# Hybrid attention and retention layer on one core: merged probabilities in dilation 1, and two reordered seams

## The chip, the core and the metric

The kernel runs on one core of a Trainium2 chip. Its engines work side by side, each through a queue of its own in order: TensorE (PE, matrix products and transposes; PEld is its weight load), VectorE (DVE), ScalarE (ACT), GpSimd (POOL) and SyncE (SP, which here only issues DMA transfers). The metric is the device time of one execution in microseconds (us).

## The reference

One decoder layer over 4096 positions of width 1024: RMSNorm, one input projection, two groups of heads, SiLU gates, one output projection, a residual add and a final RMSNorm. The part that the change touches is the dilated attention:

```python
ATTN_HEADS = 8; ATTN_HEAD_DIM = 64
DILATED_BRANCHES = ((128, 1), (512, 4), (2048, 16))

def dilated_branch(q, k, v, window, dilation):
    # query t attends t, t-d, t-2d, ..., t-window
    steps = window // dilation                      # 128 in each branch
    ...
    s = jnp.einsum('bhrnqd,bhrnkd->bhrnqk', qb, kb) * (Dh ** -0.5)
    dist = steps + qi - kj
    band = (dist >= 0) & (dist <= steps)            # 129 keys, over this block and the one before
    ...
    m = jnp.max(s, axis=-1, keepdims=True)
    p = jnp.exp(s - m)
    den = jnp.sum(p, axis=-1, keepdims=True)
    o = jnp.einsum('bhrnqk,bhrnkd->bhrnqd', p, vb) / den
    lse = (m + jnp.log(den))[..., 0]

def dilated_attention(q, k, v):
    ...
    w = jax.nn.softmax(jnp.stack(lses, axis=0), axis=0)
    o = jnp.sum(w[..., None] * jnp.stack(outs, axis=0), axis=0)
```

A key at distance 128 is in the band of dilation 1 (its 129th key) and in that of dilation 4 as well, and counts once in each.

Beside it stand four retention heads (chunks of 128, a running state), their GroupNorm, and `mixed = concat(silu(ga) * attn, silu(gr) * ret); mixed @ w_out`. All of it is float32; the large products are done as three products of split numbers (a high part and a rest), `mm3`.

## The kernel before

There are three phases. Phase 1 (to about 753 us) computes the projections, rotates q and k, and stores q, k, v to DRAM. Phase 2 (to about 1668 us) computes the attention and the retention. Phase 3 computes the gates, mixes the branches by their weights, projects and normalises. In phases 1 and 2 each engine's order is the order in which the code is written; in phase 3 a scheduler sets it.

**Phase 2.** A head is worked off in 24 items: four of dilation 1, eight of dilation 4, eight of dilation 16, four of dilation 1. An item is four blocks of 128 queries in two banks (halves) of two blocks. `attention()` runs over half-slots t, and `yield`s the modelled PE cost of each; the loop around it puts pieces of `filler()` (the retention and its value projection, 32 chunks) between them until the modelled time of a slot is full. Half-slot t issues, for one half of an item:

- PE: `qk_bank`, the scores S of half t (L667; two buffers in PSUM), then `t_bank`, transposes of the probabilities P of half t-2 (L704), then every second half-slot `pv_group` of the item from four half-slots before (L737);
- ACT: `o_copy` (L752), `exp_row` twice for half t-1 (L695), and for the second half of an item `t_copy`, the transposed tile T into half of `pt` (L714);
- DVE: `row_max` twice for half t (L688: adds the mask, finds the row's extreme, writes it to nm), and for the first half of an item `t_copy` (L716).

A block's P is 128 queries by 256 keys: the block before and its own. So an item has eight 128x128 transposes, less one for a block without a predecessor. `pt` has eight slots of 128x128, and there are two such tiles.

**Seam 1**, between phases 1 and 2. `store_values` multiplies v by the row scale on ACT (vo, L274) and issues its stores to DRAM from ACT's own queue (L276 to L283). The filler's first products V (L49 to L51) need a split chunk of the input: hi on ACT (L433), the rest on POOL (L434). A finished V is copied out by ACT (vch, L1036).

**Seam 2**, between phases 2 and 3. The statistics of all heads are in `raw`, and `branch_weights` turns them into weights for the three branches; heads 0 to 5 in phase 2 on DVE, heads 6 and 7 at the start of phase 3 on POOL (L516 to L528), with M and the reciprocal on DVE (L512, L513, L525) and the exponential on ACT (L518). There the weights of the output projection are split as well: hi by ACT, the rest by POOL and DVE in turn (wo, L89). The gates' first values are e (ACT, then DVE L1191), m is their split (ACT L41, DVE L42), and po the output projection.

## Time and profile before

| | us |
|---|---|
| median of 3 runs (lowest, highest) | 2422.44 (2421.32, 2423.11) |
| the profiled execution, its own time | 2423.84 |
| its span, first instruction to last | 2422.0 |
| busy in it: PE, DVE, ACT, POOL | 2340.4, 1468.1, 994.5, 732.9 |

The profile shows one execution. Busy times are sums over the span; the times from start to end are the first two rows. A group of instructions has its line, engine, operation, output and inputs by their names in the program, count, busy time and mean length in ns, then the idle time ahead of it and what ended that.

### The profile page before, as it was taken

How to read it: one execution, taken by the hardware profiler on the slowest of the kernel's cores; microseconds unless marked ns; L12 is line 12 of the kernel's file. 1: busy time of each engine (PE TensorE's matmuls, PEld its weight loads, DVE VectorE, ACT ScalarE, POOL GpSimd, SP SyncE). 2: the span in 40 equal slices, each digit the busy share in tenths (PEclk: the TensorE clock that was granted, in tenths of full speed). 3: DMA queues.
4: the chain of work that ended last, by engine and by line, in shares of the span. 5: the costliest groups of instructions: out<-in, count | busy, mean ns of one | idle time of the engine just before them, and what ended most of it. 6: DMA issues, size and time to landing. Idle time of an engine off the chain costs nothing. (4 is left out here: it accounts for less than half of the span.)

```text
span 2422.0 us, 41800 instructions
## 1 busy us (share of the span) xinstructions
PE 2340.4 (97%) x14568; PEld 1983.6 (82%) x14568; DVE 1468.1 (61%) x3908; ACT 994.5 (41%) x2870; POOL 732.9 (30%) x774
## 2 busy tenths in 40 slices
PE   7999999999997999999999999997899999999998
PEld 5778888888885888888888888876788999989997
DVE  5643443443433878787887879774665565565554
ACT  4322212212202666667666666666222222222221
POOL 5312112112112545344543535447221121121110
PEclk9999999999998999999999999999899999999999
DMA  6343343343356665758575665754676666666563
GB/s 191 129 146 125 116 142 126 118 142 124 119 170 190 162 156 138 186 128 195 136 175 149 151 168 123 184 144 157 152 167 161 144 164 159 140 159 162 144 156 92
DMA packets 404259, 362.59 MB, mean 150 GB/s; under 512 B 191848, under 2 KB 334824, under 8 KB 398928
## 3 DMA queue, kind: packets, MB, share of 16 engines
q1 hardware_dynamic: 389408, 332.91, 51.9%
q10 hardware_dynamic: 14112, 25.43, 3.4%
q8 instruction: 115, 1.88, 0.3%
q0 software_dynamic: 528, 1.58, 0.2%
q14 instruction: 96, 0.79, 0.1%
HBM read 241.18 MB, written 118.64 MB: 149 GB/s over the span
## 5 line engine op out<-in xcount | busy, mean ns | idle before, releaser
L688 DVE CUSTOM_DVE_ANT_0 S<-S,mask 128x256 f32<-128x256 f32 (+1 forms) x768 | 308.6, 402 | 159.8 <-PE S L667 124.8
L695 ACT ACTIVATE P<-S,nm 128x256 f32<-128x256 f32 (+1 forms) x768 | 337.8, 449 | 41.1 <-DVE nm L688 37.6
L51 PE MATMUL g<-h,wg 128*128 128x256 f32 x1024 | 289.9, 283 | 0.0
L704 PE MATMUL T<-ident,P 128*128 128x128 f32 x1368 | 213.7, 274 | 0.0
L50 PE MATMUL po<-wo,m 128*128 128x512 f32 x512 | 202.1, 395 | 3.0 <-POOL wo L89 2.0
L51 PEld LDWEIGHTS g<-h,wg 128*128 128x128 f32 x1024 | 196.8, 192 | 0.1
L737 PE MATMUL O<-pt,v 128*64 128x128 f32 (+1 forms) x1968 | 196.5, 326 | 0.0
L667 PE MATMUL S<-kk,qc 128*128 128x256 f32 x1024 | 187.1, 306 | 5.8 <-issue 2.6
L49 PE MATMUL po<-wohi,m 128*128 128x512 f32 x448 | 176.2, 393 | 13.3 <-ACT m L41 10.9
L1245 POOL TENSOR_TENSOR rs<-v,mhalf 128x1 f32<-128x1 f32 x32 | 17.4, 543 | 534.0 <-DVE v L1243 392.2
L667 PEld LDWEIGHTS S<-kk,qc 128*128 128x128 f32 x1024 | 149.8, 190 | 33.5 <-issue 16.9
L51 PE MATMUL po<-wohi,m 128*128 128x512 f32 x448 | 176.5, 394 | 0.0
L173 POOL TENSOR_TENSOR sq<-sq,sq 128x512 f32<-128x512 f32 x56 | 76.1, 1360 | 326.9 <-ACT sq L169 326.9
L737 PEld LDWEIGHTS O<-pt,v 128*64 128x64 f32 x1968 | 121.4, 137 | 60.8 <-issue 31.9
L41 ACT ACTIVATE m<-e 128x256 fp32r<-128x256 f32 x128 | 53.1, 417 | 285.5 <-DVE e L1191 156.4
L704 PEld LDWEIGHTS T<-ident,P 128*128 128x128 f32 x1368 | 164.4, 142 | 0.2 <-ACT wg0hi L88 0.2
L434 POOL TENSOR_TENSOR hc<-hr,hc 128x512 fp32r<-128x512 f32 x64 | 85.3, 1334 | 243.6 <-ACT hc L433 160.7
L695 ACT ACTIVATION_READ_ACCUMULATOR P<-S,nm 128x1 f32 x768 | 157.2, 205 | 0.0
L49 PE MATMUL g<-h,wg0hi 128*128 128x256 f32 x512 | 145.4, 284 | 3.3 <-ACT e L1184 3.3
L49 PE MATMUL g<-h,wg1hi 128*128 128x256 f32 x512 | 145.4, 284 | 2.8 <-ACT e L1184 2.8
L50 PE MATMUL g<-h,wg1hi 128*128 128x256 f32 x512 | 146.1, 286 | 1.7 <-DVE h L482 1.5
L50 PE MATMUL g<-h,wg0hi 128*128 128x256 f32 x512 | 145.4, 284 | 0.0
(213 smaller groups left out, 6107.0 us busy)
## 6 DMA issues: line engine op xcount, KB each, us to landing
q<-dr_q SPq DMA_DIRECT2D x128, 256.0 KB
hr<-in_xT_dram SPq DMA_DIRECT2D x64, 512.0 KB
wb<-dr_w SPq DMA_DIRECT2D x128, 192.0 KB
o<-dr_o SPq DMA_DIRECT2D x192, 128.0 KB
v<-dr_v SPq DMA_DIRECT2D x94, 256.0 KB
xt<-in_xT_dram SPq DMA_DIRECT2D x64, 256.0 KB
dr_q<-hl SPq DMA_DIRECT2D x32, 512.0 KB
dr_k<-hl SPq DMA_DIRECT2D x32, 512.0 KB
```

What stands on the lines that cost most here:

```text
L41: nc.scalar.activation(dst[:, 0], src, AF.Copy)
L49: nc.tensor.matmul(out, wh, xh, start=first and i == 0, stop=False)
L50: nc.tensor.matmul(out, wh, xl, start=False, stop=False)
L51: nc.tensor.matmul(out, wl, xh, start=False, stop=last and i == n - 1)
L173: nc.gpsimd.tensor_tensor(sums[b], sums[b], sq, ALU.add)
L434: nc.gpsimd.tensor_tensor(hc[:, :, 1, :], src, hc[:, :, 0, :].bitcast(F32), ALU.subtract)
L667: nc.tensor.matmul(s[:, j * 256 : (j + 1) * 256], qq[h, t, half][:, off : off + 128] if br == 0 else it["q"][:, t, i, :], rhs, start=(j == ...
L688: nc.vector.tensor_tensor_reduce(sv, sv, mask[:, it["br"], c0:256], 1.0, BIG, ALU.add, ALU.min, accum_out=nm[:, col : col + 1])
L695: nc.scalar.activation(it["P", i // 2][:, i % 2, c0:256], sv, AF.Exp, bias=nm[:, col : col + 1], scale=-1.0, accum_out=den[:, col : col + 1])
L704: nc.tensor.transpose(t[:, j * 128 : (j + 1) * 128], it["P", bank][:, j // 2, j % 2 * 128 : j % 2 * 128 + 128], ident)
L737: nc.tensor.matmul(o[64 * bank : 64 * bank + 64, c0 : c0 + 128 * m], vt[h, br, idx // 8][:, idx % 8, :], it["pt"][:, a : a + m, :].rearran ...
L1245: nc.gpsimd.tensor_tensor(rs, v, mhalf, ALU.pow)
```

## The change

Four things are changed.

1. In dilation 1 (all items but the last two of the last head; 62 of 64, marked `one`), the key at distance 128 is left out of the mask, and counts twice in dilation 4 instead (its mask there is -log 2, as scores are negated). A query then has 128 keys, and at each position within a block only one of the two, the key in the block before or in its own, is allowed: so `merge` adds the two 128x128 parts of P into one, on DVE for the first bank and on POOL for the second. `t_merged` transposes the four merged parts into one tile T. `t_apart` takes them apart: ACT copies T to the even slots of `pt` (L755 in the changed kernel), DVE multiplies T by a triangle into the odd slots (L757), and POOL multiplies the even slots in place by the other triangle (L758). pv of a merged item stands two half-slots later, that of the item behind it one. P has five buffers instead of three.
2. The triangles are made at the start of phase 2 out of the mask, with one transpose.
3. Seam 1: two of the last vo tiles come from another pool, the hi parts of chunks 0 and 1 are made on DVE, chunk 0's earlier, and vch of chunks 0 and 1 is copied by DVE.
4. Seam 2: the branch weights of heads 6 and 7 are computed on DVE and spread over the first three steps of the split of wo; an unused Silu at the end of phase 2 has ACT's table loaded earlier.

```diff
@@ store_values (seam 1)
             if b + 1 == NBLK and i >= 2:
-                vf = op.tile([128, 2, BLK], F32, tag="hl", name="vo1")[:, 0, :]
+                vf = xp.tile([128, BLK], F32, tag="x", name="vo1")
@@ the last block of phase 1 (seam 1): moved from behind store_values(b, 0, p) to ahead of the splits of w2
+                ahead["hch"] = {0: [split_h_chunk(nc, hcp, raw, 0, j, nc.vector) for j in range(2)]}
+                ahead["hr"] = load_x_chunk(nc, hcp, io, 1)
...
-                    if i == 0:
-                        ahead["hch"] = {0: [split_h_chunk(nc, hcp, raw, 0, j) for j in range(2)]}
-                        ahead["hr"] = load_x_chunk(nc, hcp, io, 1)
@@ split_h_chunk
-def split_h_chunk(nc, pool, t, c, i):
+def split_h_chunk(nc, pool, t, c, i, hi=None):
 
     hc = pool.tile([128, KT // 2, 2, 128], F32R, tag=f"hc{(2 * c + i) % 3}", name="hc2")
     src = t[:, KT // 2 * i : KT // 2 * (i + 1), :]
-    nc.scalar.activation(hc[:, :, 0, :], src, AF.Copy)
+    if hi:
+        hi.tensor_copy(hc[:, :, 0, :], src)
+    else:
+        nc.scalar.activation(hc[:, :, 0, :], src, AF.Copy)
     nc.gpsimd.tensor_tensor(hc[:, :, 1, :], src, hc[:, :, 0, :].bitcast(F32), ALU.subtract)
     return hc
@@ branch_weights (seam 2): every engine.tensor_tensor becomes nc.vector.tensor_tensor
-def branch_weights(nc, dr, raw, M, h0, h1, engine=None):
+def branch_weights(nc, dr, raw, M, h0, h1):
...
-    engine.tensor_tensor(den, nm, den, ALU.mult)
+    nc.vector.tensor_tensor(den, nm, den, ALU.mult)
@@ phase2, setup
-        pp = pool("p2p", 3)
+        pp = pool("p2p", 5)
...
+        nc.vector.tensor_scalar(mask[:, 0, :128], mask[:, 0, 128:], -1.0, BIG, ALU.mult, ALU.add)
+        for half, far in ((0, 128), (1, 0)):
+            mv = mask[:, 1, half * 128 : half * 128 + 128]
+            nc.gpsimd.affine_select(
+                out=mv,
+                in_=mv,
+                compare_op=ALU.not_equal,
+                fill=-float(np.log(2.0)),
+                base=32 - far,
+                pattern=[[32, 4], [1, 4], [4, 8]],
+                channel_multiplier=-1,
+            )
+
+        tri = cp.tile([128, 2, 128], F32, name="tri2")
+        nc.vector.tensor_scalar(tri[:, 1, :], mask[:, 0, 128:], 0.0, None, ALU.is_equal)
+        trit = psT.tile([128, 512], F32, tag="T", name="tri2")
+        nc.tensor.transpose(trit[:, :128], tri[:, 1, :], ident)
+        nc.vector.tensor_copy(tri[:, 0, :], trit[:, :128])
+        nc.vector.tensor_scalar(tri[:, 1, :], trit[:, :128], -1.0, 1.0, ALU.mult, ALU.add)
@@ phase2, new helpers
+        def merge(it, bank):
+
+
+            a = 1 if it["blocks"][2 * bank][1] == 0 else 0
+            P = it["P", bank]
+            (nc.gpsimd if bank else nc.vector).tensor_tensor(P[:, a:, 128:], P[:, a:, 128:], P[:, a:, :128], ALU.add)
+
+        def t_merged(it):
+
+            t = psT.tile([128, 512], F32, tag="T", name="T2")
+            for i in range(4):
+                nc.tensor.transpose(t[:, i * 128 : (i + 1) * 128], it["P", i // 2][:, i % 2, 128:], ident)
+            it["T"] = t
+
+        def t_apart(it):
+            t = it["T"].rearrange("p (b q) -> p b q", b=4)
+            pt = it["pt"].rearrange("p (b t) q -> p b t q", t=2)
+            nc.scalar.activation(pt[:, :, 0, :], t, AF.Copy)
+            low, up = (tri[:, i].unsqueeze(1).broadcast_to([128, 4, 128]) for i in range(2))
+            nc.vector.tensor_tensor(pt[:, :, 1, :], t, low, ALU.mult)
+            nc.gpsimd.tensor_tensor(pt[:, :, 0, :], pt[:, :, 0, :], up, ALU.mult)
+
@@ phase2, items and attention()
+                it["one"] = br == 0 and not (h == H - 1 and gi >= len(groups) - 2)
+
+                it["slot"] = 2 * len(items) + (6 if it["one"] else 5 if items and items[-1]["one"] else 4)
...
+                im = im if im and im["one"] and not bm else None
+                i2 = i2 if i2 and not i2["one"] else None
+                if im:
+                    t_merged(im)
+                    cost += 4 * TRN
                 if i2:
                     cost += t_bank(i2, b2) * TRN
-                if 0 <= g < len(items):
-                    pv_group(items[g])
-                    cost += pv_cost(items[g])
-                if 0 <= gp < len(items):
-                    o_copy(items[gp])
+                for itp in by_slot.get(t - 1, ()):
+                    o_copy(itp)
+                for itp in by_slot.get(t, ()):
+                    pv_group(itp)
+                    cost += pv_cost(itp)
                 if i1:
                     exp_row(i1, 2 * b1)
                     exp_row(i1, 2 * b1 + 1)
+                    if i1["one"]:
+                        merge(i1, b1)
+                if im:
+                    t_apart(im)
@@ filler(), retention's value projection
-                        nc.scalar.activation(res[c]["vch"], pv, AF.Copy, scale=ahead["rs"][:, c : c + 1])
+                        if c < 2:
+                            nc.vector.tensor_scalar(res[c]["vch"], pv, ahead["rs"][:, c : c + 1], None, ALU.mult)
+                        else:
+                            nc.scalar.activation(res[c]["vch"], pv, AF.Copy, scale=ahead["rs"][:, c : c + 1])
@@ pacing
-            872 + TRN * (8 - sum(it["blocks"][2 * i][1] == 0 for i in range(2))) + pv_cost(it) for it in items[: len(groups)]
+            872 + TRN * (4 if it["one"] else 8 - sum(it["blocks"][2 * i][1] == 0 for i in range(2))) + pv_cost(it)
+            for it in items[: len(groups)]
@@ end of phase 2
+            if t == n + 1:
+
+                nc.scalar.activation(ahead["junk"], ahead["mhalf"], AF.Silu)
@@ start of phase 3 (seam 2)
-            for _ in branch_weights(nc, dr, raw, M, 6, 8, nc.gpsimd):
-                pass
...
+            weights = branch_weights(nc, dr, raw, M, 6, 8)
             for j in range(7):
+                for _ in range((5, 3, 4, 0, 0, 0, 0)[j]):
+                    next(weights, None)
                 wo7.split(j, None if j % 2 else nc.gpsimd)
```

Lines of the changed kernel differ: scores L687, row maxima L708, exponentials L715, transposes L724 (L749 for merged items), vch on DVE L1093, weight splits L88, mm3 L48 to L50.

**DVE in a stretch with dilation 1** (near the boundary of heads 2 and 3; S are the scores, nm the row's extremes, the rows with nm alone read out an accumulator). Before:

```order
L688 ISA S2_6912,nm2_5477<-S2_6912,mask2_5378 128x256 [waits PE_49,Activation_49]
L688 ISA nm2_5477 128x1
L688 ISA S2_6912,nm2_5477<-S2_6912,mask2_5378 128x256 [waits DVE_49]
L688 ISA nm2_5477 128x1
L716 COPY pt0_5390<-T2_6917 128x512 [waits PE_49]
L688 ISA S2_6937,nm2_5477<-S2_6937,mask2_5378 128x256 [waits PE_49,Activation_49]
L688 ISA nm2_5477 128x1
L688 ISA S2_6937,nm2_5477<-S2_6937,mask2_5378 128x256 [waits DVE_49]
```

After (stm, mv, rs and qc belong to the filler or to the next item's queries):

```order
L743 TENSOR_TENSOR P2_7039<-P2_7039 128x2x128 [waits Activation_49,Pool_49]
L708 ISA S2_7073,nm2_6965<-S2_7073,mask2_5379 128x256 [waits PE_49]
L708 ISA nm2_6965 128x1
L708 ISA S2_7073,nm2_6965<-S2_7073,mask2_5379 128x256 [waits DVE_49]
L708 ISA nm2_6965 128x1
L1052 BN_AGGR mv2_7025<-bs2_7024 128x2 x4
L1053 TENSOR_SCALAR rs2_7026<-mv2_7025 128x4 [waits DVE_49]
L988 TENSOR_TENSOR stm2_7103<-Rs2_7096,decay2_5381 128x512 [waits PE_49]
L663 COPY qc2_7109<-q2_10_6715 128x512 [waits DMAHW3_49,DMAHW7_49,DMAHW2_49,DMAHW0_49]
L757 TENSOR_TENSOR pt0_5404<-T2_7118,tri2_5398 128x4x128 [waits Activation_49]
L708 ISA S2_7113,nm2_6965<-S2_7113,mask2_5379 128x256
L708 ISA nm2_6965 128x1
```

The copy of a T tile, which waits for PE, is gone; ahead of the row maxima stands a merge or a multiplication, and each waits for ACT.

**ACT at the same place** (P are the probabilities, os the copy of a finished output, hc a chunk of the filler). Before:

```order
L695 ACTIVATE P2_6878,den2_5478<-S2_6879,nm2_5477 128x256 [waits DVE_49,Activation_49]
L695 ACTIVATE P2_6878,den2_5478<-S2_6879,nm2_5477 128x256
L752 ACTIVATE os2_6947<-O2_6922 128x256 [waits DMAHW5_49,DMAHW4_49,PE_49]
L695 ACTIVATE P2_6911,den2_5478<-S2_6912,nm2_5477 128x256 [waits DVE_49,Activation_49]
L695 ACTIVATE P2_6911,den2_5478<-S2_6912,nm2_5477 128x256
L714 ACTIVATE pt0_5390<-T2_6942 128x512 [waits PE_49]
L1016 ACTIVATE on2_6721<-Rt2_6959 128x512 [waits DMAHW2_49,PE_49]
L695 ACTIVATE P2_6936,den2_5478<-S2_6937,nm2_5477 128x256 [waits DVE_49,Activation_49]
```

After:

```order
L715 ACTIVATE P2_7039,den2_6966<-S2_7040,nm2_6965 128x256 [waits DVE_49,Activation_49]
L715 ACTIVATE P2_7039,den2_6966<-S2_7040,nm2_6965 128x256
L434 ACTIVATE hc2_7085<-hr2_6832 128x4x128
L715 ACTIVATE P2_7072,den2_6966<-S2_7073,nm2_6965 128x256 [waits DVE_49,Activation_49]
L715 ACTIVATE P2_7072,den2_6966<-S2_7073,nm2_6965 128x256
L755 ACTIVATE pt0_5404<-T2_7118 128x4x128 [waits PE_49,Pool_49]
L794 ACTIVATE os2_7146<-O2_7123 128x256 [waits DMAHW2_49,DMAHW1_49,PE_49]
L715 ACTIVATE P2_7112,den2_6966<-S2_7113,nm2_6965 128x256 [waits DVE_49,Activation_49]
```

The copy into pt stands behind the second pair of exponentials, as before, but it now takes a merged T, DVE's multiplication waits for it, and it waits for POOL.

**PE at the start of phase 2** (mm1 is phase 1's last product, V the filler's first). Before:

```order
L50 MATMUL mm1_5273<-w1v7_634,h1_4621 128x512
L51 MATMUL mm1_5273<-w1vhi_128,h1_4621 128x512
L49 MATMUL V2_5418<-w2hi_4948,hc2_5199 128x512 [waits Activation_49]
L50 MATMUL V2_5418<-w20_5142,hc2_5199 128x512 [waits DVE_49]
L51 MATMUL V2_5418<-w2hi_4948,hc2_5199 128x512 [waits Pool_49]
```

After:

```order
L49 MATMUL mm1_5273<-w1v7_634,h1_4621 128x512
L50 MATMUL mm1_5273<-w1vhi_128,h1_4621 128x512
L600 MATMUL tri2_5400<-ident2_5374,tri2_5398 128x128 [waits DVE_49,Pool_49]
L48 MATMUL V2_5432<-w2hi_4948,hc2_5138 128x512 [waits Activation_49]
L49 MATMUL V2_5432<-w20_5150,hc2_5138 128x512
```

A transpose of the triangle, which waits for DVE and POOL, stands first.

**DVE at the start of phase 3.** Before:

```order
L512 TENSOR_TENSOR M3_5322<-raw3_5321 32x256 [waits DMAHW5_49,DMAHW4_49]
L513 TENSOR_TENSOR M3_5322<-M3_5322,raw3_5321 32x256 [waits DMAHW6_49,DVE_49]
L525 RECIPROCAL M3_5322<-M3_5322 32x256 [waits Pool_49]
L89 TENSOR_TENSOR wo1_17884<-wo2_17752,wohi_17734 128x1024 [waits DMAHW2_49,DMAHW1_49,DMAHW3_49,PE_49,Activation_49]
L89 TENSOR_TENSOR wo3_17982<-wo4_17756,wohi_17734 128x1024 [waits DMAHW3_49,DMASW0_49,DMAHW4_49,Activation_49,Pool_49]
L89 TENSOR_TENSOR wo5_18109<-wo6_17760,wohi_17735 128x1024 [waits DMAHW5_49,DMAHW6_49,Activation_49,Pool_49]
```

After:

```order
L512 TENSOR_TENSOR M3_5322<-raw3_5321 32x256 [waits DMAHW5_49,DMAHW4_49]
L513 TENSOR_TENSOR M3_5322<-M3_5322,raw3_5321 32x256 [waits DMAHW6_49,DVE_49]
L516 TENSOR_TENSOR raw3_5321<-M3_5322,raw3_5321 32x256 [waits DVE_49]
L516 TENSOR_TENSOR raw3_5321<-M3_5322,raw3_5321 32x64x4
L516 TENSOR_TENSOR raw3_5321<-M3_5322,raw3_5321 32x16x16
L520 TENSOR_TENSOR raw3_5321<-raw3_5321 32x768 [waits DMAHW7_49,DMAHW0_49,Activation_49]
L522 TENSOR_TENSOR M3_5322<-raw3_5321 32x256 [waits DVE_49]
L523 TENSOR_TENSOR M3_5322<-M3_5322,raw3_5321 32x256 [waits DVE_49]
L525 RECIPROCAL M3_5322<-M3_5322 32x256 [waits DVE_49]
L88 TENSOR_TENSOR wo1_17778<-wo2_17651,wohi_17633 128x1024 [waits DMAHW1_49,DMASW7_49,DMAHW2_49,Activation_49,Pool_49]
L528 TENSOR_TENSOR raw3_5321<-raw3_5321,M3_5322 32x256 [waits DVE_49]
L528 TENSOR_TENSOR raw3_5321<-raw3_5321,M3_5322 32x256 x2
```

The operations between M and the reciprocal, which POOL had, stand in DVE's queue; the first of wo stands behind the reciprocal as before, and three of the weights' operations behind that.

More of the change, by code (lines that the diff above doesn't have):

```diff
@@ L21 @@
 HS = 5
-WAITG = 3
 REST = 6500.0
@@ L494, in gate_products @@
     )
-def branch_weights(nc, dr, raw, M, h0, h1, engine=None):
-    engine = engine or nc.vector
+def branch_weights(nc, dr, raw, M, h0, h1):
     ps = slice(16 * h0, 16 * h1)
@@ L515, in branch_weights @@
     for br in range(3):
-        engine.tensor_tensor(nat(nm, br), shp(M, br), nat(nm, br), ALU.subtract)
+        nc.vector.tensor_tensor(nat(nm, br), shp(M, br), nat(nm, br), ALU.subtract)
         yield
@@ L527, in branch_weights @@
     for br in range(3):
-        engine.tensor_tensor(shp(den[:, br, :], br), nat(nm, br), shp(M, br), ALU.mult)
+        nc.vector.tensor_tensor(shp(den[:, br, :], br), nat(nm, br), shp(M, br), ALU.mult)
         yield
@@ L821, in attention @@
             nh = 2 * len(items)
+            by_slot = {}
+            for it in items:
+                by_slot.setdefault(it["slot"], []).append(it)
             def half(t):
@@ L832, in attention @@
                 i2, b2 = half(t - 2)
-                g = (t - 4) // 2 if t % 2 == 0 else -1
-                gp = (t - 5) // 2 if t % 2 else -1
+                im, bm = half(t - 4)
                 if it and b == 0:
@@ L1049, in filler @@
                     if k == 0 and 1 <= c < NCH:
-                        hch[c].append(split_h_chunk(nc, hcp, hraw.pop(c), c, 1))
+                        hch[c].append(split_h_chunk(nc, hcp, hraw.pop(c), c, 1, nc.vector if c < 2 else None))
                     if k == HL and 1 <= c < NCH - 1:
@@ L1355, in body @@
             tc.nc.sync.dma_start(ahead["rgain"], io["ret_gain"])
+            ahead["junk"] = rawp.tile([128, 1], F32, name="junk3")
             ahead["mhalf"] = rawp.tile([128, 1], F32, name="mhalf3")
```

8 lines of the change are left out of this document (4 added, 4 removed).

## The prediction

> **What bounds the kernel now.** I read the page first, for the shares of the engines.
>
> ```profile
> span 2422.0 us, 41800 instructions
> PE 2340.4 (97%) x14568; PEld 1983.6 (82%) x14568; DVE 1468.1 (61%) x3908; ACT 994.5 (41%) x2870; POOL 732.9 (30%) x774
> ```
>
> TensorE is busy nearly all the time, so anything taken off it should count. But the share is a mean over three phases, so I next read the table of stretches over the places that the change touches: seven stretches of eight items each (an item is two half-slots, four query blocks) with dilation 1, the last four of one head and the first four of the next. The first row and the sum (busy time of each engine, then PE's clock):
>
> ```profile
> 873.90:909.90 36.00, 36.00 (x289) 30.24 (x288) 27.62 (x102) 24.30 (x82) 12.37 (x14) 1.00 0.75 181
> ...
> sum 251.50, PE 251.31 PEld 211.71 DVE 188.64 ACT 178.37 POOL 82.90; mean PE 35.90 PEld 30.24 DVE 26.95 ACT 25.48 POOL 11.84
> ```
>
> PE is busy for 251.31 of 251.50 us at full clock (the 1.00), so it is the bound there; 251.5 / 56 = 4.49 us per item. DVE has 75%, ACT 71%: neither is full, but both are full enough that the order in which they wait for one another matters. So I read the groups of instructions by line and shape (busy time, mean ns of one), and then the timeline inside one such stretch.
>
> ```profile
> L714 ACT ACTIVATE pt<-T 128x512 f32<-128x512 f32 x128 | 76.9, 601 | 10.6 <-PE T L704 10.3
> L932 DVE TENSOR_TENSOR stm<-Rs,decay 128x512 f32<-128x512 f32 x32 | 22.0, 688 | 17.3 <-PE Rs L923 17.1
> L1202 DVE TENSOR_TENSOR a<-a,u 128x256 f32<-128x256 f32 x64 | 27.0, 421 | 0.6
> L434 POOL TENSOR_TENSOR hc<-hr,hc 128x512 fp32r<-128x512 f32 x64 | 85.3, 1334 | 243.6 <-ACT hc L433 160.7 <-DVE on L1002 20.5 <-DMA q<-dr_q 20.4
> L1191 DVE SCALAR_TENSOR_TENSOR e<-rt,rgain,e 128x256 f32<-128x256 f32 x64 | 45.1, 707 | 21.6 <-ACT e L1184 16.7 <-DMA rt<-dr_ret 4.8
> ```
>
> ```profile
> 1102.59 0.47 ACT L695 ACTIVATE P<-S,nm 128x256 f32<-128x256 f32 x1
> 1102.77 0.60 PE L704 MATMUL T<-ident,P 128*128 128x128 f32 x4
> 1103.08 0.43 DVE L688 CUSTOM_DVE_ANT_0 S<-S,mask 128x256 f32<-128x256 f32 x1 [0.57 <-PE S L667]
> 1103.20 0.38 PE L942 MATMUL Rk<-ident,rk 128*128 128x128 f32 x2
> ...
> 1103.48 0.61 ACT L714 ACTIVATE pt<-T 128x512 f32<-128x512 f32 x1
> 1103.60 0.43 DVE L688 CUSTOM_DVE_ANT_0 S<-S,mask 128x256 f32<-128x256 f32 x1
> ...
> 1103.95 0.14 DVE L688 DVE_READ_ACCUMULATOR2_ANT nm<- 128x1 f32 x1
> ...
> 1104.19 0.48 ACT L695 ACTIVATE P<-S,nm 128x256 f32<-128x256 f32 x1
> ...
> 1105.01 0.20 ACT L695 ACTIVATION_READ_ACCUMULATOR P<-S,nm 128x1 f32 x1
> ```
>
> What to see: DVE starts the row maxima of one half (1103.08) while ACT is still at the exponentials of the half before (from 1102.59). They overlap: DVE waits only for PE's scores, and every copy out of T waits only for PE's transposes.
>
> **The change part by part.**
>
> *Fewer transposes.* A merged item has 4 transposes instead of 8 (7 in a head's first group). By the order of both, 240 fewer. Four in the timeline run from 1102.77 to the next PE operation at 1103.20, 0.43 us, some 0.109 each (0.43 / 4): 240 x 0.109 = 26.2 us less PE work, all of it on the path wherever PE is the bound. The filler (retention) is paced by the cost model, so this is spread over 192 items: 0.14 each. A dilation-1 item whose bound is PE would take 4.49 - 0.14 = 4.35 us.
>
> *Copies, merges and multiplications.* ACT had one copy of a T tile per item (L714, 0.60) and has one still, so nothing. POOL gets a merge of 256 columns and a multiplication in place over 512 (L434, 1.33; the merge is half as wide, so at most that): under 2.7 us per merged item. With the 33% that it has, POOL stays below a full item; its results are wanted a slot or two later, since pv moves from slot 2i+4 to 2i+6. I cost that at nothing; the cover is those two slots, and the five instead of three P buffers. DVE gets a merge of 256 columns with both inputs in SBUF (nearest L1202, 0.42) and a multiplication out of PSUM over 512 (nearest L932, 0.69) in place of a copy of the same size.
>
> *The new waits on DVE, which decide.* By the order of the changed kernel, in a merged item's odd half-slot DVE's merge (L743) stands ahead of the next row maxima, and waits for ACT's exponentials of the half before. In the even half-slot DVE's multiplication by the triangle (L757) stands ahead of the row maxima, and waits for ACT's copy (L755), which stands on ACT's queue behind the exponentials of the half before. ACT's exponentials wait for DVE's row maxima. So where DVE and ACT now overlap, they would alternate, once round per item:
> - row maxima to exponentials: 1103.08 to 1104.19, 1.11;
> - exponentials to the copy behind them: 1102.59 to 1103.48, 0.89; the copy 0.61;
> - hand-over ACT to DVE: 0.05 (ACT's vo below ends at 758.50, PE's V starts at 758.55);
> - multiplication: 0.69, the next starting 0.08 before its end (L688 at 1103.60 lasts 0.43, its successor starts 0.35 later): 0.61;
> - row maxima again 1.11; exponentials to their last result, 1104.19 to 1105.21, 1.02; hand-over 0.05; merge 0.42 - 0.08 = 0.34.
>
> Sum 5.79 us against 4.35: 1.44 more for each of the 62 merged items, 89 us. PE can run ahead by two score buffers only, so each of the 8 stretches (the first four items, seven boundaries of heads, two at the end) hides about 1 us once, 8 in all: +81. Bounds of the one unknown size, the merge: L1202's 0.42, taken as the nearest in shape and kind; above, the factor by which such an operation grew beside POOL. In the seam below, two L1191 took 2.96 us while POOL worked from 1699.34 to 1702.54, against 2 x 0.707: 2.1 times. At that, the merge costs 0.46 more, 62 x 0.46 = +28. Below, the wait is free if other work on DVE hid it: 0.
>
> The section "Who interferes with whom" of the Trainium skill's page "SBUF — State Buffer" says that a DVE instruction with two SBUF inputs and a GpSimd instruction that reads SBUF lock each other out for a whole instruction. That speaks against the merge on DVE; the 2.96 us row agrees in direction, though it shows a stretch and no full block (a full block until 1702.54 would have put the end near 1703.95, and it came at 1703.21). By that rule, with POOL's retention work (a third of the time) in the way, the merge waits up to 1.33, about 0.44 in the mean: 2488 in place of 2461.
>
> *Setup and seam 1* (start of phase 2):
>
> ```profile
> 754.10 0.78 POOL L572 DMA_DIRECT2D mask<-in_masks_dram  x1
> mask<-in_masks_dram POOLq DMA_DIRECT2D x1, 384.0 KB, 6.7
> 757.81 0.69 ACT L274 ACTIVATE vo<-mm,rs_all 128x512 f32<-128x512 f32 x1 [7.54 <-DMA dr_k<-hl]
> 758.55 0.79 PE L49 MATMUL V<-w2hi,hc 128*128 128x512 f32 x1 [4.93 <-ACT vo L274]
> 777.71 0.80 PE L49 MATMUL V<-w2hi,hc 128*128 128x512 f32 x1 [11.51 <-ACT vch L1036]
> 783.91 0.63 ACT L433 ACTIVATE hc<-hr 128x512 fp32r<-128x512 f32 x1 [5.74 <-DMA hr<-in_xT_dram]
> ```
>
> Now the triangle's transpose stands first on PE and needs the mask, which lands at 754.10 + 6.7 = 760.8; with two small DVE operations V starts near 761.7 instead of 758.55, 3.1 later. On POOL the two affine selects wait for the mask too, with the retention's first loads queued behind them: those are wanted after chunk 1, so nothing. Against it, vch of chunk 0 leaves ACT, whose queue is full of value stores, for DVE: the 11.51 us wait shrinks to about 0.8. That is 10.7 - 3.1 = 7.6, and a little more at full clock; but ACT's split of chunk 2 still waits for its load ahead of the exponentials. I take 8 us off (4 to 10).
>
> *Seam 2* (start of phase 3):
>
> ```profile
> 1669.82 1.28 ACT L1184 ACT_TABLE_LOAD   x1 [3.30 <-DMA dr_o<-os]
> 1675.22 1.04 DVE L513 TENSOR_TENSOR M<-M,raw 32x256 f32<-32x256 f32 x1
> 1679.39 0.84 ACT L518 ACTIVATE raw<-raw 32x768 f32<-32x768 f32 x1 [2.57 <-POOL raw L516]
> 1686.54 1.75 DVE L525 RECIPROCAL M<-M 32x256 f32<-32x256 f32 x1 [10.28 <-POOL M L523]
> 1688.32 1.22 DVE L89 TENSOR_TENSOR wo<-wo,wohi 128x1024 fp32r<-128x1024 f32 x1
> 1699.34 3.20 POOL L89 TENSOR_TENSOR wo<-raw,wohi 128x1024 fp32r<-128x1024 f32 x1 [1.39 <-DVE wo L89]
> 1700.25 2.96 DVE L1191 SCALAR_TENSOR_TENSOR e<-rt,rgain,e 128x256 f32<-128x256 f32 x2
> L89 POOL TENSOR_TENSOR wo<-wo,wohi 128x1024 fp32r<-128x1024 f32 x3 | 7.0, 2349 | 1.6 <-DVE wo L89 1.4
> L516 DVE TENSOR_TENSOR raw<-M,raw 96x256 f32<-96x256 f32 x3 | 2.4, 813 | 0.0
> L522 DVE TENSOR_TENSOR M<-raw 96x256 f32<-96x256 f32 x1 | 1.7, 1654 | 0.0
> ```
>
> Today the weights of heads 6 and 7 go through POOL, DVE waits 10.28 us for them, and its second e (1700.25) and PE behind it stall. All on DVE: M is ready at 1676.26, three L516 to 1678.7, ACT's exponential to 1679.5, then the product, the two sums and their like (two L522's length at most, 3.3, and half as much again for L520) to about 1683.2 to 1684.5, the reciprocal to about 1685, wo of step 1 to 1686.2 instead of 1689.54. From there POOL and DVE alternate through wo 2 to 5: 2 x 2.35 + 2 x 1.22 = 7.1, so e starts at 1693.3 instead of 1700.25, 7.0 earlier. The preloaded table saves up to 1.28 more, where PE waits for the first e. I take 8 off (5 to 11). The weights' stores go later on SP's queue than the loads of rt, but the weights themselves are ready earlier than now.
>
> *Sum.* +81 - 26 - 8 - 8 = +39. The profiled run took 2423.84, 1.84 around its span of 2422.0, and lies 1.40 above the median of the runs, 2422.44: 2463 by the profiled run, 2461 by the median, which I forecast.
>
> **The rivals.** All from the same sum; a net of zero needs 0.81 more than 4.35 per merged item ((26 + 16 + 8) / 62), a round of some 5.2 us.
>
> 1. *PE stays the bound* (the other side: faster). The waits cost nothing where DVE and ACT have slack elsewhere in the item. For it: DVE at 75% and ACT at 71%. Against: both of DVE's waits stand directly ahead of the row maxima that ACT waits for, and two score buffers don't cover 1.4 us per item again and again. It decides if the round is below 4.35. Then only the gains are left: 2422 - 26 - 16 = 2380.
> 2. *Half a chain.* If the multiplication need not wait for ACT's copy into the same pt tile, or the copy finds a gap between exponentials, 0.66 falls out: a round of 5.13, 62 x 0.78 - 8 = +40, net -2: about 2421. For it: the two write different halves of the tile. Against: the order gives the wait on ACT there.
> 3. *POOL lengthens the merge*, as bounded above: +28, 2489. For it, the L1191 row; against, that POOL's own multiplication begins together with DVE's and ends long before the merge.
> 4. *The clock falls* in stretches where PE idles. The stretch around the first seam shows it:
>
> ```profile
> 753.00:791.00 38.00, 21.56 (x95) 17.46 (x94) 6.25 (x23) 6.86 (x18) 16.59 (x21) 0.73 0.69 202
> ```
>
> There PE was busy for 57% and was granted 0.73 of its clock. In the forecast it would be busy for 4.35 / 5.79 = 75%. At half clock PE's 4.35 would be 8.7 per item; in one stretch in eight that is some 8 x 2.9 = 23 us more: about 2485 to 2510.
>
> **How the numbers follow.** Forecast (round of 5.5 to 6.0, 2443 to 2475 with the seams' bounds) 0.56; rival 1 0.12; rival 2, with rounds of 4.9 to 5.4 (2406 to 2437), 0.12; rival 3 0.14; rival 4 0.06. A difference under 0.2% (4.8 us) is about what a measurement of this kernel can't tell from none. Rival 1 and a third of rival 2 are faster, 0.16; a quarter of rival 2 and little else is no change, 0.04; slower 0.80. The range leaves out rival 1, the low end of rival 2 and the worst of rivals 3 and 4: 2412 to 2495; the forecast's own is 2443 to 2475.
>
> **What the profile after would show.** Right: in the same stretches PE's busy share falls to about 75%, an item takes 5.5 to 6 us, PE's idle time ahead of its scores (S, L687) is released by ACT's exponentials, and DVE has new idle time ahead of the merge and the multiplication released by ACT, some 62 x 2 times. L749 and L724 together have 1128 transposes. The stretches with dilation 4 and 16 get shorter by 0.14 per item. V starts near 761.7, and again for chunk 1 near 770 instead of 777.71; in phase 3 the e that starts at 1700.25 comes some 7 us earlier after M than now. Wrong would be: PE at 97% in those stretches (rival 1); idle time only ahead of the merge (rival 2); a merge above 0.6 us in the mean (rival 3); a clock below 1 there (rival 4). What would make it wrong most easily is ACT's or DVE's queue running ahead at a place where I have them wait, since the sum counts each link in full.

## The result, and the profile after

| | us |
|---|---|
| before, median of 4 runs (lowest, highest) | 2422.61 (2421.32, 2423.11) |
| after, median of 4 runs (lowest, highest) | 2487.95 (2484.29, 2489.70) |
| ratio after to before, 95% interval | 1.0268 (1.0253 to 1.0282) |
| the profiled execution after, its span | 2484.29, 2482.5 |

The change makes the kernel 65 us slower; the forecast was 2461, with 2488 inside the stated range (2412 to 2495), but above the 2443 to 2475 of the forecast's own mechanism. The profiled execution is the fastest of the four, and its span is 60.5 us longer than before's. The page's first two lines:

```profile
span 2482.5 us, 41541 instructions
PE 2341.0 (94%) x14329; PEld 1963.8 (79%) x14329; DVE 1517.2 (61%) x3989; ACT 991.5 (40%) x2865; POOL 855.5 (34%) x891
```

PE has 239 instructions fewer (240 transposes off, the triangle's one added), and yet its share of the span falls from 97 to 94%: it waits. The table of stretches over the same seven places as before, each from the first of a head's last four items to the fourth of the next head (first row, and the sum):

```profile
878.30:922.40 44.10, 35.85 (x265) 28.57 (x265) 30.46 (x110) 25.12 (x85) 29.74 (x31) 1.00 0.79 173
...
sum 310.40, PE 257.09 PEld 201.67 DVE 211.20 ACT 177.21 POOL 190.66; mean PE 36.73 PEld 28.81 DVE 30.17 ACT 25.32 POOL 27.24
```

Cut at the same scores, eight items took 35.6 us before (249.5 / 7) and take 44.3 now (310.4 / 7), with PE busy for 83%, at full clock in six of the seven, and no other engine above 68%. An engine that is full would explain the loss; none is. What PE and DVE wait for, in the views of waits (total, times, longest, us); the first row is before's, the others after's:

```profile
PE S L667 <- ACT P L695: 6.9, 8, 2.3
```

```profile
PE S L687 <- ACT P L715: 60.0, 84, 3.3
PE O L779 <- POOL pt L758: 5.2, 7, 0.9
DVE P L743 <- ACT P L715: 61.0, 54, 2.7
DVE pt L757 <- ACT pt L755: 44.4, 37, 3.7
```

PE's wait for the score buffers that ACT's exponentials free went from 6.9 to 60.0 us: 53 of the 60.5. DVE's two new waits are the merge behind the exponentials and the multiplication behind ACT's copy. One round of the loop in the timeline, with the start and length of each operation:

```profile
1140.86 0.69 DVE L757 TENSOR_TENSOR pt<-T,tri 128x512 f32<-128x512 f32 x1 [0.87 <-ACT pt L755]
1141.47 0.42 DVE L708 CUSTOM_DVE_ANT_0 S<-S,mask 128x256 f32<-128x256 f32 x1
...
1142.57 0.47 ACT L715 ACTIVATE P<-S,nm 128x256 f32<-128x256 f32 x1 [1.47 <-DVE nm L708]
...
1143.05 1.28 POOL L758 TENSOR_TENSOR pt<-pt,tri 128x512 f32<-128x512 f32 x1
...
1143.64 0.74 PE L687 MATMUL S<-kk,q 128*128 128x256 f32 x4 [1.03 <-ACT P L715]
1143.69 0.92 DVE L743 TENSOR_TENSOR P<-P 128x256 f32<-128x256 f32 x1 [1.22 <-ACT P L715]
1144.27 1.33 POOL L663 CAST qc<-q 128x512 fp32r<-128x512 f32 x1
1144.53 0.42 DVE L708 CUSTOM_DVE_ANT_0 S<-S,mask 128x256 f32<-128x256 f32 x1
...
1145.63 0.47 ACT L715 ACTIVATE P<-S,nm 128x256 f32<-128x256 f32 x1 [2.04 <-DVE nm L708]
...
1146.54 0.60 ACT L755 ACTIVATE pt<-T 128x512 f32<-128x512 f32 x1
1146.71 0.62 DVE L663 CAST qc<-q 128x512 fp32r<-128x512 f32 x1
...
1147.24 0.69 DVE L757 TENSOR_TENSOR pt<-T,tri 128x512 f32<-128x512 f32 x1
1147.85 0.43 DVE L708 CUSTOM_DVE_ANT_0 S<-S,mask 128x256 f32<-128x256 f32 x1
```

From the row maxima at 1141.47 to the same ones of the next item at 1147.85 each step starts where the one before ends: maxima, 1.10 to the exponentials, 1.12 to the merge, 0.84 to the maxima, 1.10 to the exponentials, 0.91 to the copy, 0.70 to the multiplication, 0.61 to the maxima: 6.38 us. ACT is idle before each pair of exponentials until DVE's maxima are done (1.47 and 2.04), and DVE before the merge until ACT's exponentials are (1.22). The multiplication at 1140.86 waited for ACT's copy as well (0.87); ahead of the one at 1147.24 DVE's own retention work and a cast of queries filled that time. PE's scores at 1143.64 wait for the exponentials.

The merge took 0.92 there and not 0.42. POOL's multiplication, which began at 1143.05, ended at 1144.33; the merge ended 0.28 later, at 1144.61. The groups by shape:

```profile
L743 DVE TENSOR_TENSOR P<-P 128x256 f32<-128x256 f32 x54 | 29.7, 549 | 54.2 <-ACT P L715 51.6 <-POOL qc L663 2.4
L757 DVE TENSOR_TENSOR pt<-T,tri 128x512 f32<-128x512 f32 x62 | 42.7, 689 | 45.0 <-ACT pt L755 44.4
L743 POOL TENSOR_TENSOR P<-P 128x256 f32<-128x256 f32 x62 | 49.1, 792 | 62.5 <-ACT P L715 56.8 <-issue 3.4 <-POOL qbd L967 1.5
L758 POOL TENSOR_TENSOR pt<-pt,tri 128x512 f32<-128x512 f32 x62 | 81.6, 1316 | 4.8 <-ACT pt L755 4.1 <-PE O L779 0.5
```

The merge has a mean of 0.55; the multiplication, which reads T from PSUM, is at 0.69 in the mean, though 57 of the 62 began while POOL was at work.

The first seam (the rows with an idle time are those that waited):

```profile
762.60 0.45 PE L600 MATMUL tri<-ident,tri 128*128 128x128 f32 x1 [7.65 <-DVE tri L598]
770.79 0.59 DVE L962 CAST qbd<-rq 64x256 fp32r<-64x256 f32 x2 [8.34 <-DMA rq<-dr_r]
776.20 0.43 DVE L432 CAST hc<-hr 128x512 fp32r<-128x512 f32 x1 [4.09 <-DMA hr<-in_xT_dram]
776.54 0.74 DVE L1093 TENSOR_SCALAR vch<-V,rs_all 128x512 f32<-128x512 f32 x1
777.34 0.79 PE L48 MATMUL V<-w2hi,hc 128*128 128x512 f32 x1 [7.68 <-DVE vch L1093]
783.24 0.64 PE L687 MATMUL S<-kk,q 128*128 128x256 f32 x4
```

The copy vch has left ACT's queue and stands in DVE's, behind a cast that waits for rq and behind a split that waits for chunk 1's load. Chunk 1 starts at 777.34 where it was 777.71.

### The profile page after: what moved, and what is told of

Its sections match the earlier page's. It is cut to its first block, busy times and chain, and to the rows that moved or that the text cites. A ratio compares the mean times of both kernels' runs of the same rounds, so it can differ in the third digit from the quotient of the medians.

```text
span 2482.5 us, 41541 instructions
## 1 busy us (share of the span) xinstructions
PE 2341.0 (94%) x14329; PEld 1963.8 (79%) x14329; DVE 1517.2 (61%) x3989; ACT 991.5 (40%) x2865; POOL 855.5 (34%) x891
## 5 line engine op out<-in xcount | busy, mean ns | idle before, releaser
L715 ACT ACTIVATE P<-S,nm 128x256 f32<-128x256 f32 (+1 forms) x768 | 337.5, 448 | 183.3 <-DVE nm L708 180.6
L708 DVE CUSTOM_DVE_ANT_0 S<-S,mask 128x256 f32<-128x256 f32 (+1 forms) x768 | 307.1, 401 | 90.2 <-PE S L687 62.3
L50 PE MATMUL g<-h,wg 128*128 128x256 f32 x1024 | 290.9, 284 | 0.0
L687 PE MATMUL S<-kk,qc 128*128 128x256 f32 x1024 | 191.2, 311 | 23.3 <-ACT P L715 18.7
L50 PEld LDWEIGHTS g<-h,wg 128*128 128x128 f32 x1024 | 197.2, 193 | 0.0
L687 PEld LDWEIGHTS S<-kk,qc 128*128 128x128 f32 x1024 | 148.7, 192 | 59.5 <-ACT P L715 27.8
L48 PE MATMUL po<-wohi,m 128*128 128x512 f32 x448 | 178.5, 398 | 7.1 <-ACT m L40 6.6
L50 PE MATMUL po<-wohi,m 128*128 128x512 f32 x448 | 177.0, 396 | 0.3 <-DVE m L41 0.3
L715 ACT ACTIVATION_READ_ACCUMULATOR P<-S,nm 128x1 f32 x768 | 155.8, 203 | 0.0
L1247 ACT ACTIVATE e<-g 128x256 f32<-128x256 f32 x128 | 48.2, 378 | 254.5 <-PE g L50 235.9
L48 PE MATMUL g<-h,wg0hi 128*128 128x256 f32 x512 | 145.4, 284 | 2.0 <-ACT e L1247 2.0
L48 PE MATMUL g<-h,wg1hi 128*128 128x256 f32 x512 | 145.6, 285 | 1.3 <-ACT e L1247 1.2
L724 PE MATMUL T<-ident,P 128*128 128x128 f32 x880 | 139.6, 274 | 0.0
```

The lines of the kernel that those rows point to most:

```text
L48: nc.tensor.matmul(out, wh, xh, start=first and i == 0, stop=False)
L50: nc.tensor.matmul(out, wl, xh, start=False, stop=last and i == n - 1)
L687: nc.tensor.matmul(s[:, j * 256 : (j + 1) * 256], qq[h, t, half][:, off : off + 128] if br == 0 else it["q"][:, t, i, :], rhs, start=(j == ...
L708: nc.vector.tensor_tensor_reduce(sv, sv, mask[:, it["br"], c0:256], 1.0, BIG, ALU.add, ALU.min, accum_out=nm[:, col : col + 1])
L715: nc.scalar.activation(it["P", i // 2][:, i % 2, c0:256], sv, AF.Exp, bias=nm[:, col : col + 1], scale=-1.0, accum_out=den[:, col : col + 1])
L724: nc.tensor.transpose(t[:, j * 128 : (j + 1) * 128], it["P", bank][:, j // 2, j % 2 * 128 : j % 2 * 128 + 128], ident)
```

## The experiments

Every ratio is to the kernel before, measured beside it on the same chip, with its 95% interval; on the chips of these runs the kernel before took 2427 to 2430 us. The middle columns are from one profile of each kernel, by the starts of the scores: the time of the 64 dilation-1 items, that of the 128 others, and that from the first to the last scores, in us. A profiled execution can lie some us off its kernel's median: that of rm_before_merge is 6.9 above it, that of plain_best 3.8 above, that of merged_best 3.7 below.

| kernel | ratio (interval) | dilation 1 | others | first to last scores |
|---|---|---|---|---|
| before | 1 | 289.3 | 584.7 | 874.0 |
| after | 1.0268 (1.0253 to 1.0282) | 357.2 | 586.9 | 944.2 |
| dil_only | 1.0303 (1.0286 to 1.0320) | 356.6 | 585.0 | 941.6 |
| seams_only | 0.9962 (0.9948 to 0.9975) | 288.6 | 583.8 | 872.5 |
| rm_before_merge | 1.0134 (1.0115 to 1.0154) | 327.2 | 594.8 | 921.9 |
| rm_before_mult | 1.0083 (1.0066 to 1.0100) | 320.4 | 586.7 | 907.1 |
| rm_first | 1.0008 (0.9996 to 1.0021) | 305.2 | 580.6 | 885.8 |
| pv_later | 1.0057 (1.0036 to 1.0079) | 305.9 | 590.7 | 896.5 |
| dve_mults | 0.9983 (0.9970 to 0.9996) | 295.8 | 584.0 | 879.8 |
| gather_late | 0.9943 (0.9926 to 0.9961) | 291.7 | 580.9 | 872.6 |
| seam1 | 0.9968 (0.9956 to 0.9980) | 303.2 | 581.8 | 885.1 |
| merged_best | 0.9917 (0.9896 to 0.9939) | 292.4 | 578.6 | 871.0 |
| plain_best | 0.9921 (0.9906 to 0.9936) | 291.2 | 586.1 | 877.3 |
| merged_best2 | 0.9902 (0.9887 to 0.9918) | 294.2 | 577.8 | 872.0 |

**Which part loses.** Merging switched off, all else as changed:

```diff
-                it["one"] = br == 0 and not (h == H - 1 and gi >= len(groups) - 2)
+                it["one"] = False
```

> The changed kernel with no item merged (eight transposes per item and the copies of before); the new masks, the triangles and both seams stay. Theory: the loss is all in the merged items; seam 2 gives about 9 us (in the changed kernel the time from the last scores to the end is 755.1 us against 764.3), seam 1 nothing (first scores at 783.2 against 783.7): 2410 to 2416 us. Rival: the new masks, setup or seams carry a part of the loss: above 2420 us. Prediction on record: both seams 16 us, 2407 us.

0.9962, some 9 us below before. The masks, the triangles and the seams carry none of the loss. The reverse, with merging kept and both seams written as before (vo from "hl", splits and vch on ACT, branch weights on POOL, no early table):

> The changed kernel with merged items and their setup, but both seams as before. If the parts add up, the 1.0268 of the changed kernel and the 0.9962 of the seams alone: 1.030 to 1.0315, some 2496 us against 2422.6. The setup's transpose at the head of PE's queue then stands beside the old first seam, where V waited until 758.6 for vo and 777.7 for vch: if it costs nothing there, 1.029 to 1.030.

1.0303, as the sum of the parts has it (1.0306). Within the intervals, seams and merging don't act on each other.

**Is it the loop between DVE and ACT?** Three orders of DVE's queue, with the same instructions. In rm_first the row maxima of half t go ahead of both the merge and the multiplication:

```diff
                 if i1:
                     exp_row(i1, 2 * b1)
                     exp_row(i1, 2 * b1 + 1)
-                    if i1["one"]:
-                        merge(i1, b1)
+                if it:
+                    row_max(it, 2 * b)
+                    row_max(it, 2 * b + 1)
+                if i1 and i1["one"]:
+                    merge(i1, b1)
                 if im:
                     t_apart(im)
                 if i2 and b2:
                     t_copy(i2, b2)
-                if it:
-                    row_max(it, 2 * b)
-                    row_max(it, 2 * b + 1)
```

> The changed kernel, with the row maxima of half t issued on DVE ahead of the merge and of the triangle multiplication. Theory (DVE and ACT alternate once round per merged item): the round is cut in both places, a merged item takes what PE needs, about 4.35 us in place of the 5.58 that the changed kernel shows in its 64 dilation-1 items (357 us together), so some 79 us come back and a few more from the items behind each stretch: 2390 to 2410 us, and PE's wait for ACT's exponentials ahead of the scores falls from 60 us to under 10. Rival A (POOL sets the pace: shared port, or merges and multiplications too slow): stays above 2465 us. Rival B (DVE is simply too full there): 2440 to 2465 us.

1.0008: 63 of the 65 us are gone by the order of one queue alone. That is the theory's direction, and nearly all of the loss; it isn't 2390 to 2410, for 2430 was measured on this chip's scale of 2429, between the theory's range and that of rival B (2440 to 2465). PE's waits and the sum over the seven stretches:

```profile
PE S L687 <- ACT P L715: 18.6, 24, 3.4
PE O L779 <- POOL pt L758: 9.6, 13, 1.2
PE T L749 <- POOL P L743: 3.6, 6, 0.9
```

```profile
sum 259.30, PE 246.21 PEld 201.68 DVE 222.51 ACT 181.98 POOL 183.70; mean PE 35.17 PEld 28.81 DVE 31.79 ACT 26.00 POOL 26.24
```

The wait for the exponentials falls from 60.0 to 18.6, not below 10; DVE is now at 86% and POOL at 71% of these stretches. One cut alone, ahead of the merge (t_apart stays ahead of row_max, merge goes behind):

> The changed kernel, with the row maxima ahead of the merge alone; the multiplication still stands ahead of them. Theory: what is left of the round is row maxima 1.11, exponentials to copy 0.89, copy 0.61, hand-over 0.05, multiplication 0.61 and the other half's row maxima 0.87, 4.14 us, under PE's 4.35, so one cut gives nearly all back: 2390 to 2415 us. Rival C (the two waits add up, each for itself: DVE waited 61 us ahead of the merge and 44 ahead of the multiplication): only the merge's part comes back, 2425 to 2440 us. Rival A (POOL): above 2465 us.

And ahead of the multiplication (merge stays ahead of row_max, t_apart goes behind):

> The changed kernel, with the row maxima ahead of the multiplication alone; the merge still stands ahead of them. Theory: what is left of the round is 1.11 + 1.02 + 0.05 + 0.34 + 0.87 = 3.39 us, under PE's 4.35: 2388 to 2412 us. Rival C: the multiplication's part alone comes back, 2440 to 2455 us. Rival A: above 2465 us.

1.0134 and 1.0083: this is nearer to rival C's shape than to the theory's. The second lies in C's range; the first (2461 on this chip, 2455 on the scale of 2422.6) lies above C's 2425 to 2440. That edit does one thing more than it was meant to: in the even half-slots it puts POOL's merge behind POOL's multiplication, and PE's transposes waited 10.5 us for that merge where they waited 0.3 in the changed kernel. So its 33 us are less than DVE's wait alone would give. The other cut gives 45, and 78 is not far above the 63 that both give: each wait costs largely for itself, with a part in common. DVE's waits in the two kernels, from their first to their last scores, show the one that was left in place:

```profile
DVE pt L757 <- ACT pt L755: 45.2, 34, 3.3
DVE P L743 <- ACT P L715: 12.0, 40, 0.7
```

```profile
DVE P L743 <- ACT P L715: 36.0, 46, 2.7
DVE pt L757 <- ACT pt L755: 9.3, 17, 0.9
```

With the merge's wait cut, the multiplication waits as long as it did (45.2 against 44.4); with the multiplication's cut, the merge waits 36.0 where it waited 61.0. My rounds of 4.14 and 3.39 us were too short to be true. In rm_before_merge's trace 53 rounds, from one multiplication to the next, have a mean of 5.5 us: maxima to exponentials took 1.52 for 1.11, exponentials to the copy 1.44 for 0.89, the copy to the multiplication 0.94 for 0.66. The sum had no place for the retention's operations and the casts that stand in DVE's queue, nor for POOL's merge ahead of the transposes; how much each adds was not taken apart. That a round without them would hide entirely under PE was argued, and fell.

**What is left.** First, more time for POOL: pv another half-slot later, three pt tiles.

```diff
-        PT = [c2.tile([128, 8, 128], F32, name=f"pt{i}") for i in range(2)]
+        PT = [c2.tile([128, 8, 128], F32, name=f"pt{i}") for i in range(3)]
...
-                it["slot"] = 2 * len(items) + (6 if it["one"] else 5 if items and items[-1]["one"] else 4)
+                it["slot"] = 2 * len(items) + (7 if it["one"] else 6 if items and items[-1]["one"] else 4)
```

> As rm_first, with pv of a merged item in half-slot 2i+7 in place of 2i+6 (the next item's in 2i+6 in place of 2i+5) and three pt tiles in place of two. If only the time that POOL's multiplication has before pv is short (PE's 9.6 us ahead of the outputs): 5 to 10 us less than rm_first, a ratio to before of 0.997 to 0.999. If POOL's and DVE's lock and load set the pace: no change, 1.000 to 1.002.

1.0057, slower than rm_first by 12 us, which neither case expected. The dilation-1 items are unchanged (305.9), the others lose 10. PE's wait for POOL's multiplication is gone from the list, so the lateness of POOL's result was not the price; its wait for the exponentials went from 18.6 to 25.2, and why the later pv costs is not settled. Second, POOL's work taken away: both triangle multiplications on DVE straight out of PSUM, no copy on ACT, both merges on POOL.

```diff
-            nc.scalar.activation(pt[:, :, 0, :], t, AF.Copy)
...
-            nc.gpsimd.tensor_tensor(pt[:, :, 0, :], pt[:, :, 0, :], up, ALU.mult)
+            nc.vector.tensor_tensor(pt[:, :, 0, :], t, up, ALU.mult)
...
-            (nc.gpsimd if bank else nc.vector).tensor_tensor(P[:, a:, 128:], P[:, a:, 128:], P[:, a:, :128], ALU.add)
+            nc.gpsimd.tensor_tensor(P[:, a:, 128:], P[:, a:, 128:], P[:, a:, :128], ALU.add)
```

> As rm_first, with T taken apart by two DVE multiplications straight out of PSUM (no copy by ACT, no multiplication on POOL), and both merges on POOL. rm_first still takes 4.77 us per dilation-1 item (305 us in 64) where PE needs 4.35. Theory D (POOL is what is left: PE waits 9.6 us ahead of the outputs for POOL's multiplication and 3.6 ahead of the transposes for its merge, and DVE's operations with two SBUF inputs and its casts are locked out while POOL works): 10 to 25 us less than rm_first, a ratio to before of 0.990 to 0.997. Rival E (DVE is full: 222.5 of 259.3 us in the seven stretches, plus 56 x 0.61 = 34, less 54 merges of 0.63): no faster than rm_first, a ratio of 1.000 to 1.008.

0.9983, 6 us better than rm_first: between the two cases, with an interval that only reaches into theory D's. POOL was a part of what was left, the smaller one. A dilation-1 item falls from 4.77 to 4.62 us (295.8 / 64). It is also the first merged kernel clearly not slower than before. What stays sits at the end of a stretch; there the timeline shows

```profile
1233.30 1.19 DVE L1052 TENSOR_SCALAR rs<-mv 128x4 f32<-128x4 f32 x1
1233.98 0.74 PE L687 MATMUL S<-kk,q 128*128 128x256 f32 x4
...
1235.00 0.63 DVE L663 CAST qc<-q 128x512 fp32r<-128x512 f32 x1
1235.55 0.42 DVE L708 CUSTOM_DVE_ANT_0 S<-S,mask 128x256 f32<-128x256 f32 x1
...
1237.72 0.74 PE L687 MATMUL S<-kk,qc 128*128 128x256 f32 x4 [1.61 <-ACT P L715]
```

Scores that were ready near 1234.7 get their maxima at 1235.55, behind the retention's rs (lengthened to 1.19) and a cast of queries for the next dilation, and the next scores start 1.61 late. In gather_late the cast goes behind the maxima:

```diff
-                soon_it, sb = half(t + 4)
-                if soon_it and sb == 0:
-                    gather_q(soon_it)
...
                     row_max(it, 2 * b)
                     row_max(it, 2 * b + 1)
+                soon_it, sb = half(t + 4)
+                if soon_it and sb == 0:
+                    gather_q(soon_it)
```

> As dve_mults, with DVE's gather of the next dilation's queries (the casts into qc, 0.6 us alone and up to 1.6 beside POOL) issued behind the row maxima of its half-slot in place of ahead of them. What is left in dve_mults stands at the end of a dilation-1 stretch and on its first dilation-4 item (5.2, 4.9 and 5.9 us against 4.4 to 4.6 within), where PE waits for ACT's exponentials and these for row maxima that stand behind casts and retention work on DVE. Theory F (queue order at DVE): 4 to 8 us less than dve_mults, a ratio to before of 0.995 to 0.9967. Rival (DVE is full there, the order among its operations is all the same): no change, 0.9975 to 0.999.

0.9943, 10 us better, a little more than expected: again only the place in DVE's queue.

**The first seam.** Chunk 1's load goes to POOL's queue, the triangle's transpose and the affine selects into half-slot 1:

```diff
-                ahead["hr"] = load_x_chunk(nc, hcp, io, 1)
+                ahead["hr"] = load_x_chunk(nc, hcp, io, 1, nc.gpsimd)
...
+                if t == 1:
...
+                    trit = psT.tile([128, 512], F32, tag="T", name="tri2")
+                    nc.tensor.transpose(trit[:, :128], tri[:, 1, :], ident)
```

> As rm_first, with the first seam opened: chunk 1's load is issued on POOL's queue instead of SP's (where it stood behind stores until 765.9), and the triangle's transpose and the two affine selects are moved into half-slot 1. In the changed kernel V started at 762.6 behind the triangle, and the wait for vch (7.7 us, until 777.3) was DVE's queue standing behind the landing of rq (770.8) and of chunk 1 (776.2). Theory: V starts when vo is out, near 755 to 756; rq lands near 764; chunk 1 starts 5 to 9 us earlier, first scores 5 to 10 us earlier, and the time falls by as much: a ratio of 0.996 to 0.999. Rival: the start of phase 2 is set by something else (mask, value stores on ACT's queue, the load of chunk 2 ahead of the exponentials), and under 3 us come back: 0.9995 to 1.001.

```profile
757.26 0.50 PE L48 MATMUL V<-w2hi,hc 128*128 128x512 f32 x1 [1.34 <-ACT vo L273]
767.90 0.79 PE L48 MATMUL V<-w2hi,hc 128*128 128x512 f32 x1 [4.91 <-DVE vch L1093]
776.43 0.81 PE L671 MATMUL S<-kk,q 128*128 128x256 f32 x4
```

0.9968 against rm_first's 1.0008: some 10 us, with the first scores at 776.4 instead of 784.4 in rm_first. The wait for vch falls from 7.68 to 4.91; what is left of it again stands behind loads, since DVE waits until 763.45 for the mask and until 765.94 for rq. The two moves of this run are not told apart.

**Together.** All that helped, with and without merged items:

> gather_late and the opened first seam of seam1 together. If they add up (seam1 took 0.0040 off rm_first): 0.991 to 0.993 of before, 2408 to 2413 us on this chip's scale of 2429.

> seam1 with no item merged: eight transposes per item as before, and both seams, the first one opened. seams_only stood at 0.9962 of before; with 0.0040 of seam1: 0.991 to 0.9935. If merged items can be made to pay at all, merged_best is below this one; if it is not, the 26 us of PE work that merging takes off are used up by the work that it puts on DVE and POOL even in the better order.

0.9917 and 0.9921: the two can't be told apart. In merged_best the transposes of the first dilation-4 items still wait 9.2 us for DVE's second multiplication to free a T tile, so the gather goes to the end of the half-slot:

> merged_best, with the gather of queries at the very end of its half-slot, behind the triangle multiplications as well. In merged_best the second dilation-4 item still takes 5.9 us: PE's transposes wait (9.2 us together) for DVE's second multiplication to free a T tile, and that stands behind a cast of 0.64. Theory F: some 3 to 6 us less than merged_best, a ratio to before of 0.989 to 0.991, below plain_best's 0.9921. Rival: DVE is full there and nothing comes back: 0.991 to 0.9925.

0.9902, 24 us below before; its interval overlaps both others. It beats the kernel before and the changed one. The wait for T fell to 4.4 us, but PE's wait for the exponentials rose from 14.7 to 20.0, and the time from the first to the last scores did not fall (871.0 and 872.0): that the last move helped is not shown. Nor is it shown that merging itself pays: 872.0 against plain_best's 877.3 us is a difference of 5.3, and plain_best's profiled execution lies 3.8 above its median.

## Why the prediction was right, and where it was off

*Side and mechanism: right.* The loop was forecast from the order of the queues, and its links are in the timeline after: 1.10 twice for 1.11, 0.91 for 0.89, the copy with its hand-over 0.70 for 0.66, the multiplication 0.61 for 0.61, exponentials with their hand-over 1.12 for 1.07, and the merge 0.84 for 0.34. Rivals 1 and 2 fell: PE is not the bound (83% busy), and DVE waits ahead of both the merge and the multiplication. Rival 4 is small: the clock in those stretches is 1.00 in six of seven rows, and between the first and the last scores there are five windows of 3.4 us at half clock (near 806, 1158, 1274, 1550 and 1612) against three before (1493, 1626, 1650); two more cost at most 2 x 1.7 us by estimate.

*Excess of merged items: about right, in part by luck.* +81 over PE's need of 4.35 was forecast. The 64 items took 357.2 us against 64 x 4.35 = 278, so +79. The rounds themselves were longer than the forecast's 5.79. Over the 53 rounds between one merged item and the next, the medians of the links add up to 5.82, but the mean round is 6.2: POOL held up some merges, and DVE's retention work and casts stood ahead of some multiplications (the link from the copy is 0.79 in the mean for 0.66). Against that, the first two items of a stretch at a head's end took only 4.5 and 4.8 us in the mean. The round reaches PE late, and leaves it as late, in the items behind.

*The total: luck as well.* 2488 is also the time that the prediction gave for a merge locked out by POOL. The lock-out is real, but it cost the merges some 7 us and not 27; the other 20 come from the items behind the stretches and from the first seam, as below.

*The 26 us of transposes: right away from the stretches, lost behind them.* (0.43 / 4 is 0.108, not 0.109, which leaves the 26 as it is.) I let all items get 0.14 shorter. The 128 others took 586.9 against 584.7 us, where the step has 128 x 0.14 = 18 less. The dilation-16 items did shorten (35.2 to 36.4 us for eight in heads 0 to 5, against 36.6 to 37.6), by 0.16 each over all heads, but the dilation-4 ones became longer (36.4 to 37.4 against 34.6 to 36.0): the first item behind a stretch takes 6.2 us in the mean where it took 4.4, and the second 4.9 for 4.4. The round runs on into them, since the last two multiplications of a stretch stand ahead of their row maxima. I had taken the ends of stretches as a gain of 1 us each.

*Seam 1: the step that failed.* I took 8 us off; the first scores came 0.5 us earlier (783.2 against 783.7). I wrote that the loads queued behind the affine selects on POOL "are wanted after chunk 1, so nothing". DVE's cast of rq is issued ahead of vch, and so is the split of chunk 1, whose load SP issued at 765.9 behind stores. A wait that leaves ACT's queue enters DVE's. seam1 bears it out: with both loads issued earlier, and the triangle's transpose out of the way, the first scores come 8 us earlier, which is what I had forecast.

*Seam 2: about right.* 8 us forecast. From the last scores to the end of the span it was 764.3 us before (2422.0 - 1657.7) and is 755.1 now, 9.2 less. The e that starts at 1700.25 before came 25.0 us behind DVE's M (L513), and comes 18.9 behind it now (1746.04 and 1764.98): 6.1 earlier, for the 7 forecast. The wait ahead of po went from 10.9 to 6.6, before and after:

```profile
PE po L49 <- ACT m L41: 10.9, 1, 10.9
```

```profile
PE po L48 <- ACT m L40: 6.6, 1, 6.6
```

*Rival 3, POOL and the merge: real, small.* 54 merges of 0.55 in place of 0.42 are 7 us, not 28. Where POOL was at work when a merge came, the merge ended 0.28 behind POOL's end, as in the round above. That is the full lock-out which the Trainium skill's page "SBUF — State Buffer", section "Who interferes with whom", describes for an instruction with two SBUF inputs; the prediction had doubted it from a single row. That row shows it too, once it is taken apart: of the two e, the first ran from 1700.25 to 1702.81 and ended 0.27 behind POOL's 1702.54, and the second took 0.47, not the mean of 0.707. The multiplication, with one input in PSUM, was never longer.

By place, from the scores' starts in the two profiles: dilation-1 items +67.9 where the forecast has 81 - 64 x 0.14 = +72; the others +2.2 for -18; seam 1 -0.5 for -8; seam 2 -9.2 for -8. That is +60.4 for +38 in all: the forecast fell short by the items behind the stretches (20 us) and by the first seam (7.5).

## What to carry to other kernels

Before an instruction is put on a queue, look at what it waits for and what is queued behind it: two engines that each wait for the other ahead of work that the other needs take turns, though neither is full (here DVE at 68% and ACT at 57%). The cure was the order of one queue, 63 of 65 us, with not one instruction less. A copy that is moved off a blocked queue takes over the waits of the queue that it is moved to.
